# State-space rounds of a hybrid encoder block: the output products of one round stand right ahead of the table turns of the next

## The chip, the core and the metric

The kernel runs on one core of one Trainium2 chip. The metric is the device time in microseconds of one execution; three runs of the kernel before gave 892.14 (median), 893.0 and 890.85. The engines are TensorE (PE: matmuls and transposes), the vector engine (DVE), ScalarE (ACT), GpSimd (POOL), and SP, whose queue issues nearly all DMAs. Each engine works through its own instructions in their order; semaphores let one wait for another.

## The reference

One layer over a sequence of 1024 tokens of width 1024, float32 throughout: a combined input projection, a differential attention branch, a bidirectional state-space branch (S5), gates, and an output projection. The part that the change touches:

```python
proj = h @ w_in
q, k, v, z_a, u, z_s, g_a, g_s = jnp.split(proj, IN_OFFSETS, axis=-1)
...
bu_re = jnp.einsum('bsgh,gph->sbgp', uf, bb_re)     # 32 groups of 16 channels, 64 complex states
bu_im = jnp.einsum('bsgh,gph->sbgp', uf, bb_im)
_, _, x_re, x_im = lax.associative_scan(combine, (a_re, a_im, bu_re, bu_im), reverse=reverse, axis=0)
y = (jnp.einsum('sbgp,ghp->bsgh', x_re, c_re) - jnp.einsum('sbgp,ghp->bsgh', x_im, c_im))
...
y = forward(ug) + backward(ug) + d_skip * u
y = jax.nn.gelu(y)
y = y * jax.nn.sigmoid(y @ w_glu + b_glu)
ssm_branch = (y * jax.nn.silu(z_s)) @ w_up_ssm
```

The kernel forms the scan in chunks of 8 tokens: within a chunk by a product with a Toeplitz table `m`, across chunks by a scan on the vector engine.

## The kernel before

The state-space part runs in 8 rounds (i = 0 to 7) of 4 channel groups each, in `ssm_main`. At the same time TensorE has a large store of other work, the rest of the input projection. The function `drive` mixes the two by hand: `ssm_main` is a generator that yields numbers, and after each yield `drive` runs steps of the other work (the filler, `s1_fill`) until their costs add up to the number. One filler step is three wide matmuls (128x512, `mm`, L222), costed 0.66. The order on every engine's queue is just the order in which this code is written out; nothing rearranges it.

A round consists of:

- `stage_a`, `stage_rot` (vector engine): tables `cb` and `rr` for the next round; `stage_u` (SP): four DMAs that load `ut`, the inputs of the next round (L960). `ut` has 2 buffers, so the one for round i+1 takes the buffer of round i-1.
- `stage_c`: 8 products `w` on TensorE (`ut` with the turned table `gt`, L1009), and six operations on the vector engine that turn them by `rr`.
- `stage_s`: four scans on the vector engine.
- `stage_e` of the round before: the output products `yp` (L1055 `ut` with `m`, L1057 `z` with `cb`), emptied by ScalarE as `ys`, and stored by four DMAs from SP.
- `stage_r`, `stage_b` for the next round: ScalarE makes `rt` and the second half of `rr`; TensorE turns `cb` in 8 transposes `tp` (L970), and ScalarE copies them to `gt`.
- `stage_d`: six operations on the vector engine that make `z` (1 buffer) out of the scans.
- `stage_k` for the next round: 8 small products `kp` (L980), `kf` on ScalarE and the vector engine, a store `kd` and four loads `m` on SP.

The filler has its own traffic. A unit is 48 matmuls, 24 for each half, and writes two PSUM buffers in turn (`ps_mm`, tag `mm`, 2 buffers); ScalarE empties each half into `side`, and after the second half SP stores it (L1123). After its first three matmuls a unit calls `w_ahead`: ScalarE and the vector engine cut the weights of the next unit into a high and a low part (`wh` on ScalarE from the raw weights `wr`, then `wl` on the vector engine), and SP loads the raw weights of the unit after that (L174, 512 KB, `wr` with 2 buffers). A unit's first matmul reads `wh`, its third `wl`. All these stand in the same queues as the rounds' own instructions, in the order of the code.

The names of the yields: YA 2.75, YB 4.8, YC 3.2, YL 3.0 (L135).

Of the kernel before, what the change touches and what calls it, by code (L numbers as in the profile page):

```python
# [66 lines left out]
def tile_hybrid_block(  # L67
# [67 lines left out]
    YF, YA, YB, YC, YL = 12.0, 2.75, 4.8, 3.2, 3.0  # L135
# [772 lines left out]
    def ssm_main(t, ye):  # L908
# [14 lines left out]
        def stage_a(i):  # L923
            g = slice(4 * i, 4 * i + 4)
            cb = hb.tile([P, 2, 4, 8, 16, 2], F32, tag="cb", bufs=3, name="cb")
            tv = hb.tile([P, 4, 8, 32], F32, tag="t1", bufs=1, name="tv")
            sc = [P, 4, 8, 32]
            bv = [bc(bct[:, q, g].rearrange("p g h x -> p g (h x)"), 2, sc) for q in range(2)]
            wv = [bc(wt[:, q, :, g].rearrange("p k g -> p g k"), 3, sc) for q in range(2)]
            cf = cb[:].rearrange("p q g t h x -> p q g t (h x)")  # L930
            outer(cf[:, 0], cf[:, 1], bv[0], bv[1], wv[0], wv[1], tv)
            st_[i] = dict(cb=cb)

        def stage_rot(i):
            g = slice(4 * i, 4 * i + 4)
            rr = hb.tile([P, 2, 4, 8, 16], F32, tag="rr", bufs=2, name="rr")
            tv = hb.tile([P, 4, 8, 32], F32, tag="t1", bufs=1, name="tv")
            sr = [P, 4, 4, 16]
            rv = [bc(ra[:, q, :, g].rearrange("p k g -> p g k"), 3, sr) for q in range(2)]
            rw = [bc(rb[:, q, :, g].rearrange("p k g -> p g k"), 2, sr) for q in range(2)]  # L940
            outer(rr[:, 0, :, 4:8], rr[:, 1, :, 4:8], rv[0], rv[1], rw[0], rw[1], tv[:, :, 0:4, 0:16])
            st_[i]["rr"] = rr

        def stage_r(i):
            d = st_[i]
            rr = d["rr"]
            rt = hb.tile([P, 4, P], F32, tag="rt", bufs=2, name="rt")
            act(rt, bc(r8[:, 4 * i:4 * i + 4], 2, [P, 4, P]), AF.Copy)
            G.memset(rt[0:64, :, 0:1], 0.0)  # L949
            G.memset(rt[64:P, :, P - 1:P], 0.0)  # L950
            for q in range(2):
                f = rr[:, q].rearrange("p g a b -> p g (a b)")
                act(f[:, :, 0:64][:, :, ::-1], f[:, :, 64:P], AF.Copy, scale=1.0 - 2.0 * q)
            d["rt"] = rt

        def stage_u(i):
            ut = hb.tile([P, 4, P], F32, tag="ut", bufs=2, name="ut")
            for q in range(4):
                r0 = (4 * i + q) * 16
                SP.dma_start(out=ut[:, q, :], in_=ud[r0:r0 + 16, :].rearrange("h (t j) -> t h j", t=T))  # L960
            st_[i]["ut"] = ut

        def stage_b(i):
            d = st_[i]
            cb = d["cb"]
            gt = hb.tile([P, 2, 4, P], F32, tag="gt", bufs=1, name="gt")
            for q in range(2):
                ps = psw.tile([P, 512], F32, tag="tp", bufs=2, name="tp")
                for c4 in range(4):
                    PE.transpose(ps[:, c4 * P:c4 * P + P], cb[:, q, c4, :, :, 0].rearrange("p t h -> p (t h)"), ident)  # L970
                act(gt[:, q], ps[:].rearrange("p (c q) -> p c q", c=4), AF.Copy)
            d.update(gt=gt)
# [30 lines left out]
        def stage_c(i):  # L1003
            d = st_[i]
            gt, ut, rr = d["gt"], d["ut"], d["rr"]
            wp = [psw.tile([P, 4, P], F32, tag="w", bufs=2, name="w") for _ in range(2)]
            for q in range(2):
                for c4 in range(4):
                    PE.matmul(out=wp[q][:, c4, :], lhsT=gt[:, q, c4, :], rhs=ut[:, c4, :], start=True, stop=True)  # L1009
            rre = rr[:, 0].rearrange("p g a b -> p g (a b)")  # L1010
            rim = rr[:, 1].rearrange("p g a b -> p g (a b)")
            wv = hb.tile([P, 2, 4, P], F32, tag="wv", bufs=1, name="wv")
            t1 = hb.tile([P, 4, P], F32, tag="t1", bufs=1, name="t1")
            mul(wv[:, 0], wp[0], rre)
            mul(t1, wp[1], rim)
            add(wv[:, 0], wv[:, 0], t1)
            mul(wv[:, 1], wp[0], rim)
            mul(t1, wp[1], rre)
            sub(wv[:, 1], wv[:, 1], t1)
            d.update(wv=wv, rre=rre, rim=rim)  # L1020

        def stage_s(i):
            d = st_[i]
            wv, rt = d["wv"], d["rt"]
            sb = hb.tile([P, 2, 528], F32, tag="sb", bufs=1, name="sb")
            rf = rt[:].rearrange("p g j -> p (g j)")
            for q in range(2):
                wf = wv[:, q].rearrange("p g j -> p (g j)")
                V.tensor_tensor_scan(out=sb[0:64, q, 2:514], data0=rf[0:64], data1=wf[0:64],
                                     initial=0.0, op0=ALU.mult, op1=ALU.add)  # L1030
                V.tensor_tensor_scan(out=sb[64:P, q, 0:512][:, ::-1], data0=rf[64:P, ::-1], data1=wf[64:P, ::-1],
                                     initial=0.0, op0=ALU.mult, op1=ALU.add)
            sv = sb[:, :, 1:513].rearrange("p q (g j) -> p q g j", g=4)
            V.memset(sv[0:64, :, :, 0:1], 0.0)
            V.memset(sv[64:P, :, :, P - 1:P], 0.0)
            d.update(sv=sv)

        def stage_d(i):
            d = st_.pop(i)
            sv, rre, rim = (d[k] for k in ("sv", "rre", "rim"))  # L1040
            z = hb.tile([P, 2, 4, P], F32, tag="z", bufs=1, name="z")
            t1 = hb.tile([P, 4, P], F32, tag="t1", bufs=1, name="t1")
            mul(z[:, 0], sv[:, 0], rre)
            mul(t1, sv[:, 1], rim)
            add(z[:, 0], z[:, 0], t1)
            mul(z[:, 1], sv[:, 1], rre)
            mul(t1, sv[:, 0], rim)
            sub(z[:, 1], z[:, 1], t1)
            return d, z

        def stage_e(i, d, z):
            ut, cb, m = d["ut"], d["cb"], d["m"]
            yp = psw.tile([P, 4, P], F32, tag="y", bufs=1, name="yp")
            for c4 in range(4):
                PE.matmul(out=yp[:, c4, :], lhsT=m[:, c4, :], rhs=ut[:, c4, :], start=True, stop=False)  # L1055
                for q in range(2):
                    PE.matmul(out=yp[:, c4, :], lhsT=cb[:, q, c4, :, :, 1].rearrange("p t h -> p (t h)"),  # L1057
                              rhs=z[:, q, c4, :], start=False, stop=(q == 1))
            ys = yo.tile([P, 4, P], F32, tag="ys", bufs=2, name="ys")
            act(ys, yp, AF.Copy if i < NH - 1 else AF.Gelu_apprx_tanh)  # L1060
            for c4 in range(4):
                r0 = (4 * i + c4) * 16
                SP.dma_start(out=yd[r0:r0 + 16, :].rearrange("h (t j) -> t h j", t=T), in_=ys[:, c4, :])
# [19 lines left out]
        for i in range(NH):  # L1083
            if 0 < i < NH - 1:
                stage_a(i + 1)
                stage_u(i + 1)
            yield YA
            if 0 < i < NH - 1:
                stage_rot(i + 1)
            yield YA  # L1090
            stage_c(i)
            yield YA
            stage_s(i)
            yield YA
            if prev is not None:
                stage_e(*prev)
            if i in (3, 5, 7):
                SP.dma_start(out=ye[:, (i - 3) // 2], in_=yd[(i - 3) // 2 * P:(i - 1) // 2 * P, :])
            yield YB
            if i + 1 < NH:  # L1100
                stage_r(i + 1)
                stage_b(i + 1)
            prev = (i,) + stage_d(i)
            if i + 1 < NH:
                stage_k(i + 1)
            yield YC
# [29 lines left out]
    yep = tc.alloc_tile_pool(name="yep", bufs=1, side="left")  # L1136
    ye = yep.tile([P, 3, S], F32, name="ye")
    drive(ssm_main(tabs, ye), s1_fill)
    pools1[0][0].release()
    pools1[1].release()  # L1140
# [762 lines left out]
```

## Time and profile before

| | |
|---|---|
| median of three runs | 892.14 us (890.85 to 893.0) |
| the profiled execution | 892.95 us |
| its span, first to last instruction | 891.1 us |
| TensorE busy | 868.5 us, 97% |
| vector engine busy | 664.2 us, 75% |
| ScalarE busy | 367.6 us, 41% |
| the rounds in the span | about 118 to 347 us |

The shares are means over the whole span; the stages differ. Within the rounds the rows of TensorE follow one another, so the timelines of the other engines have to be read against the point at which TensorE takes up what they make. A row of a timeline gives the start in microseconds from the span's start, the duration, the engine, the line, what is written and read, and in brackets the idle time before it with what ended it. Two TensorE rows can overlap, since matmuls are pipelined. An instruction of SP is an issue; the transfer goes on behind it.

### The profile page before, as it was taken

The numbers are of one execution on the slowest core, as the hardware profiler recorded it, in microseconds if no ns is written. First come the engines' busy times: TensorE is split into PE (matmuls) and PEld (weight loads), VectorE is DVE, ScalarE is ACT, GpSimd is POOL, SyncE is SP. The second block draws the span as 40 slices with busy tenths as digits, with TensorE's granted clock in tenths as the row PEclk, the third lists the DMA queues.
The fourth block names the chain that finished last, engine by engine and source line by source line (L and its number), as shares of the span: only waits on it lengthen the run. The fifth ranks groups of instructions, "written<-read, shape, count | busy, mean of one in ns | idle before, by whom it ended". The sixth has DMA issues, their size and how long they took to land.

```text
span 891.1 us, 12219 instructions
## 1 busy us (share of the span) xinstructions
PE 868.5 (97%) x4528; PEld 732.1 (82%) x4528; DVE 664.2 (75%) x1264; ACT 367.6 (41%) x613; POOL 140.8 (16%) x133
## 2 busy tenths in 40 slices
PE   5999999999999999999999999999999999999996
PEld 4878888888888888877888888888888888878886
DVE  5986999979999987678456666787677675673465
ACT  6753452122232126421245555655555653332222
POOL 1001000000000000000003723544441311350000
PEclk9899899999999999999999999999999999999998
DMA  9936133044424245569361231342343116548022
GB/s 294 306 99 189 48 119 112 23 132 133 150 83 148 71 143 161 210 252 321 95 166 48 72 95 36 83 118 60 83 118 130 59 64 221 188 167 302 28 95 95
DMA packets 106829, 118.52 MB, mean 133 GB/s; under 512 B 7683, under 2 KB 87792, under 8 KB 106770
## 3 DMA queue, kind: packets, MB, share of 16 engines
q1 hardware_dynamic: 104980, 113.03, 41.3%
q10 hardware_dynamic: 1614, 4.51, 1.3%
q8 instruction: 36, 0.59, 0.3%
q0 software_dynamic: 176, 0.20, 0.1%
q14 instruction: 23, 0.19, 0.1%
HBM read 77.93 MB, written 27.20 MB: 118 GB/s over the span
## 4 chain that ended last, share of the span: by engine, by line
PE 88%; DVE 4%; DMA 2%; ACT 2%; issue 2%; POOL 1%; ACTq 0%; SPq 0%; DVEq 0%
PE mm L222 51%; PE op L1822 9%; PE pv L1498 5%; PE tp L1487 3%; PE sc L1456 3%; PE sc L1457 3%; PE yp L1057 2%; PE w L1009 2%; PE u L831 1%; DVE acc L96 1%; PE up L1656 1%; POOL pta L78 1%; PE mm L831 1%; PE xT L767 1%; PE tp L970 1%
## 5 line engine op out<-in xcount | busy, mean ns | idle before, releaser
L222 PE MATMUL mm<-hh,wh 128*128 128x512 f32 x592 | 238.2, 402 | 0.0
L222 PE MATMUL mm<-hl,wh 128*128 128x512 f32 x592 | 232.1, 392 | 0.0
L222 PE MATMUL mm<-hh,wl 128*128 128x512 f32 x592 | 231.7, 391 | 0.0
L222 PEld LDWEIGHTS mm<-hh,wl 128*128 128x128 f32 x592 | 111.7, 189 | 24.3 <-DVE wl L78 0.5
L222 PEld LDWEIGHTS mm<-hh,wh 128*128 128x128 f32 x592 | 111.9, 189 | 22.4 <-issue 1.7
L222 PEld LDWEIGHTS mm<-hl,wh 128*128 128x128 f32 x592 | 112.0, 189 | 20.1
L99 ACT ACTIVATE e<-sc,nm 128x1024 f32<-128x1024 f32 x64 | 71.1, 1114 | 59.9 <-DVE nm L1458 59.9
L1458 DVE TENSOR_REDUCE nm<-sc 128x1 f32<-128x1024 f32 x64 | 75.4, 1219 | 16.7 <-PE sc L1457 15.4
L78 DVE TENSOR_TENSOR wtl<-tp,wth 128x512 fp32r<-128x512 f32 x64 | 41.2, 686 | 55.6 <-ACT wth L99 55.6
L99 ACT ACTIVATE wh<-wr 128x1024 fp32r<-128x1024 f32 x49 | 51.6, 1056 | 58.0 <-DMA wr<-in_w_in_dram 22.7
L99 ACT ACTIVATE side<-mm 128x512 f32<-128x512 f32 x48 | 28.7, 598 | 102.6 <-PE mm L222 60.7
L78 DVE TENSOR_TENSOR wl<-wr,wh 128x1024 fp32r<-128x1024 f32 x36 | 43.9, 1223 | 28.5 <-ACT wh L99 28.4
L1822 PE MATMUL op<-woh,mh 128*128 128x512 f32 (+1 forms) x136 | 51.3, 377 | 1.2 <-ACT mh L99 1.2
L1822 PE MATMUL op<-woh,ml 128*128 128x512 f32 (+1 forms) x136 | 51.3, 377 | 0.0
L1822 PE MATMUL op<-wol,mh 128*128 128x512 f32 (+1 forms) x136 | 51.2, 377 | 0.0
L78 POOL TENSOR_TENSOR wl<-wr,wh 128x512 fp32r<-128x512 f32 x26 | 33.0, 1292 | 114.2 <-ACT wh L99 114.1
L1456 PE MATMUL sc<-kk,qq 128*128 128x512 f32 x128 | 49.9, 390 | 0.0
L1457 PE MATMUL sc<-kk,qb 128*128 128x512 f32 x128 | 49.8, 389 | 0.0
L99 ACT ACTIVATE wth<-tp 128x512 fp32r<-128x512 f32 x64 | 34.9, 597 | 32.4 <-PE tp L1487 32.4
L96 DVE SCALAR_TENSOR_TENSOR e<-e,wm 128x1024 f32<-128x1024 f32 x32 | 43.0, 1344 | 1.1
L949 POOL MEMSET rt<- 64x4 f32 x8 | 0.8, 98 | 240.8 <-ACT rt L99 240.8
L1498 PE MATMUL pv<-wth,vh 128*128 128x256 f32 x128 | 36.2, 283 | 0.0
(378 smaller groups left out, 1724.9 us busy)
## 6 DMA issues: line engine op xcount, KB each, us to landing
wr<-in_w_in_dram SPq DMA_DIRECT2D x40, 512.0 KB
wa<-in_w_ada_dram SPq DMA_DIRECT2D x16, 512.0 KB
x<-in_x_dram SPq DMA_DIRECT2D x8, 512.0 KB
gsd<-side SPq DMA_DIRECT2D x8, 512.0 KB
gad<-side SPq DMA_DIRECT2D x8, 512.0 KB
gt<-gsd SPq DMA_DIRECT2D x8, 512.0 KB
wg<-in_w_ada_dram SPq DMA_DIRECT2D x8, 512.0 KB
pad<-pt ACTq DMA_DIRECT2D x8, 512.0 KB
```

Source lines behind the costliest of these rows:

```text
L78: (e or V).tensor_tensor(out=o, in0=a, in1=b, op=op)
L96: V.scalar_tensor_tensor(out=o, in0=a, scalar=s, in1=b, op0=op0, op1=op1)
L99: A.activation(out=o, in_=i, func=f, **kw)
L222: PE.matmul(out=ps, lhsT=a[:, k, off:off + P], rhs=r[:, k, sl], start=(n == 0), stop=(n == 3 * K - 1))
L831: PE.matmul(out=upd[b, hf], lhsT=w[:, k, :], rhs=hid[r][:, k, hf * 512:hf * 512 + 512], start=first, stop=(left[b, hf] == 0))
L1009: PE.matmul(out=wp[q][:, c4, :], lhsT=gt[:, q, c4, :], rhs=ut[:, c4, :], start=True, stop=True)
L1456: PE.matmul(out=sc[:, sl], lhsT=H["qq"][:, cc, tok], rhs=H["kk"][:, cc, sl], start=True, stop=False)
L1457: PE.matmul(out=sc[:, sl], lhsT=qb_t[g // 2][:, cc, tb], rhs=H["kk"][:, cc, sl], start=False, stop=True)
L1458: V.tensor_reduce(out=nm[:, cc:cc + 1], in_=sc, axis=AX.X, op=ALU.max, negate=True)
L1487: PE.transpose(ps[:, k, :], e[:, kt * P:kt * P + P], ident)
L1498: PE.matmul(out=ps[:, 0:256], lhsT=a[:, kt, :], rhs=r[:, kt, :], start=(n == 0), stop=(n == 23))
L1822: PE.matmul(out=ps[:, 0:n], lhsT=a[:, k, tok], rhs=r[:, k, lo:lo + n], start=(i == 0), stop=(i == 23))
```

## The change

The yield YB between `stage_e` and `stage_r`/`stage_b` is joined with the yield YA ahead of `stage_e`. The numbers stay and so does the amount of filler; the filler that ran between the two stages now runs ahead of `stage_e`, and with it everything that it puts on ScalarE, the vector engine and SP.

```diff
--- before.py
+++ after.py
@@ -1091,12 +1091,11 @@
             stage_c(i)
             yield YA
             stage_s(i)
-            yield YA
+            yield YA + YB
             if prev is not None:
                 stage_e(*prev)
             if i in (3, 5, 7):
                 SP.dma_start(out=ye[:, (i - 3) // 2], in_=yd[(i - 3) // 2 * P:(i - 1) // 2 * P, :])
-            yield YB
             if i + 1 < NH:
                 stage_r(i + 1)
                 stage_b(i + 1)
```

Since a line falls away, all later lines of the kernel move up by one: the store of `side` is L1123 before and L1122 now.

TensorE, round 1, before: the last pair of the output products of round 0, with the filler behind them.

```order
L1055 MATMUL yp<-ut,m 128x128
L1057 MATMUL yp<-z,cb 128x128 x2
L222 MATMUL mm<-hh,wh 128x512
L222 MATMUL mm<-hl,wh 128x512
L222 MATMUL mm<-hh,wl 128x512
```

TensorE, the same place now: the last pair, the turns `tp` and the products `kp` of the next round, and then filler.

```order
L1055 MATMUL yp<-ut,m 128x128
L1057 MATMUL yp<-z,cb 128x128 x2
L970 MATMUL tp<-cst,cb 128x128 x8
L980 MATMUL kp<-cb,bz 32x128 x8
L222 MATMUL mm<-hh,wh 128x512
```

The 21 filler matmuls that stood between `yp` and `tp` now stand ahead of the 8 rows of `yp`; behind `tp` nothing has changed its place.

SP's queue, round 1, before, from the load of `ut` for round 2 to the store of `kf`.

```order
L960 DMA ut<-ud 128x1x128 x4
L1123 DMA zad<-side 128x1024
L174 DMA wr<-in_w_in_dram 128x8x128
L1063 DMA yd<-ys 8x16x128 x4
L1123 DMA gsd<-side 128x1024
L174 DMA wr<-in_w_in_dram 128x8x128
L989 DMA kd<-kf 128x240
```

SP's queue, the same place now.

```order
L960 DMA ut<-ud 128x1x128 x4
L1122 DMA zad<-side 128x1024
L174 DMA wr<-in_w_in_dram 128x8x128
L1122 DMA gsd<-side 128x1024
L174 DMA wr<-in_w_in_dram 128x8x128
L1063 DMA yd<-ys 8x16x128 x4
L989 DMA kd<-kf 128x240
```

The stores of `ys` moved behind the second store of `side` and the second weight load; the load of `ut` stands first in both, and it waits there for a semaphore of TensorE.

ScalarE, round 1, before, from the emptying of the output products to that of the filler's halves.

```order
L99 ACTIVATE ys<-yp 128x512
L99 ACTIVATE side<-mm 128x512
L99 ACTIVATE wh<-wr 128x1024
L99 ACTIVATE rt<-r_959 128x512
L99 ACTIVATE rr<-rr 128x4x64 x2
L99 ACTIVATE gt<-tp 128x512 x2
L99 ACTIVATE kf<-kp 128x112
L99 ACTIVATE side<-mm 128x512 x2
```

ScalarE, the same place now.

```order
L99 ACTIVATE side<-mm 128x512 x2
L99 ACTIVATE wh<-wr 128x1024
L99 ACTIVATE ys<-yp 128x512
L99 ACTIVATE rt<-r_959 128x512
L99 ACTIVATE rr<-rr 128x4x64 x2
L99 ACTIVATE gt<-tp 128x512 x2
L99 ACTIVATE kf<-kp 128x112
L99 ACTIVATE side<-mm 128x512 x2
```

`ys` moved from ahead of the emptying of one filler half and of the cut of the weights (`wh`) to behind them.

## Rows read from the trace of the kernel before

**Rows 1.** The page, its first part: busy time, share of the span, instructions.

```profile
PE 868.5 (97%) x4528; PEld 732.1 (82%) x4528; DVE 664.2 (75%) x1264; ACT 367.6 (41%) x613; POOL 140.8 (16%) x133
```

**Rows 2.** Windows: length, busy us by engine, then TensorE's clock, DMA share, GB/s.

```profile
100.00:102.00 2.00, 2.00 (x17) 1.63 (x15) 1.91 (x17) 0.58 (x1) 0.00 (x0) 0.86 0.00 0
...
102.00:108.00 6.00, 6.00 (x20) 4.86 (x20) 6.00 (x34) 2.84 (x5) 0.00 (x0) 0.50 0.01 3
...
200.00:300.00 100.00, 100.00 (x585) 85.45 (x584) 97.38 (x139) 27.09 (x49) 0.80 (x8) 1.00 0.40 121
```

**Rows 3.** Waits of the DMA queue on SP, 115:365: total us, times, longest.

```profile
SPq L960 <- PE yp L1057: 46.1, 6, 13.0
```

**Rows 4.** Timeline of SP's DMA issues, rounds 1 and 3: start us, us, instruction.

```profile
175.99 2.44 SPq L960 DMA_DIRECT2D ut<-ud  x4
...
178.97 0.43 SPq L174 DMA_DIRECT2D wr<-in_w_in_dram  x1
...
230.58 0.43 SPq L174 DMA_DIRECT2D wr<-in_w_in_dram  x1
```

**Rows 5.** Chain that ended last: start us, us, what. Rounds 1, 3 and 6.

```profile
176.43 4.83 PE mm L222 x21
...
228.07 5.51 PE mm L222 x24
...
306.55 4.83 PE mm L222 x21
```

**Rows 6.** Timeline of ScalarE (ACT), rounds 1, 2, 3 and 6: start us, us, instruction.

```profile
176.46 0.60 ACT L99 ACTIVATE ys<-yp 128x512 f32<-128x512 f32 x1 [7.57 <-PE yp L1057]
...
184.42 1.06 ACT L99 ACTIVATE wh<-wr 128x1024 fp32r<-128x1024 f32 x1 [6.87 <-DMA wr<-in_w_in_dram]
...
187.61 0.61 ACT L99 ACTIVATE side<-mm 128x512 f32<-128x512 f32 x1
...
213.87 0.61 ACT L99 ACTIVATE side<-mm 128x512 f32<-128x512 f32 x1
...
235.59 1.06 ACT L99 ACTIVATE wh<-wr 128x1024 fp32r<-128x1024 f32 x1 [2.06 <-DMA wr<-in_w_in_dram]
...
237.68 1.06 ACT L99 ACTIVATE gt<-tp 128x512 f32<-128x512 f32 x2
...
317.93 0.61 ACT L99 ACTIVATE side<-mm 128x512 f32<-128x512 f32 x1
```

**Rows 7.** Timeline of TensorE (PE), rounds 1 to 6: start us, us, instruction.

```profile
173.50 0.38 PE L1055 MATMUL yp<-ut,m 128*128 128x128 f32 x2
...
176.18 0.49 PE L222 MATMUL mm<-hh,wh 128*128 128x512 f32 x1
...
189.01 0.39 PE L222 MATMUL mm<-hh,wh 128*128 128x512 f32 x1
...
204.98 0.39 PE L222 MATMUL mm<-hh,wl 128*128 128x512 f32 x1
...
217.21 0.39 PE L222 MATMUL mm<-hh,wh 128*128 128x512 f32 x1
...
244.06 0.49 PE L1009 MATMUL w<-ut,gt 128*128 128x128 f32 x3
...
291.39 0.39 PE L222 MATMUL mm<-hh,wl 128*128 128x512 f32 x1
...
319.13 0.39 PE L222 MATMUL mm<-hh,wh 128*128 128x512 f32 x1
```

**Rows 8.** Timeline of the vector engine (DVE), its `wl`, rounds 1 to 5.

```profile
185.51 1.23 DVE L78 TENSOR_TENSOR wl<-wr,wh 128x1024 fp32r<-128x1024 f32 x1 [6.09 <-ACT wh L99]
...
201.30 1.22 DVE L78 TENSOR_TENSOR wl<-wr,wh 128x1024 fp32r<-128x1024 f32 x1
...
237.76 1.23 DVE L78 TENSOR_TENSOR wl<-wr,wh 128x1024 fp32r<-128x1024 f32 x1
...
288.72 1.23 DVE L78 TENSOR_TENSOR wl<-wr,wh 128x1024 fp32r<-128x1024 f32 x1
```

## The prediction

> **What bounds the kernel now.** I read the page first, then the stretches, the waits, and last the timelines of the rounds. TensorE is busy 97% of the span [rows 1]; in the middle of the state-space rounds it is busy all of 200 to 300 us at full clock, with the vector engine at 97% beside it [rows 2]. So time can be won here only by making TensorE's own row of instructions shorter, and it is lost wherever TensorE comes to stand still. What matters is therefore how far its suppliers are ahead of it. The waits of the DMA queue on SP show where they start from: 46.1 us, in 6 waits, are spent at the load of `ut` until products `yp` are done on TensorE [rows 3]. `ut` has two buffers; the load for round i+1 goes into the buffer that `stage_e(i-1)` still reads. It stands in the queue ahead of the weight load, so **stage_e on TensorE opens the gate for the weights**.
>
> In round 1 that reads: `ut` issued at 175.99, 0.4 us after the last L1055 began, weights `wr` at 178.97 [rows 4]; the cut `wh` on ScalarE starts when they land, 184.42; behind it, in order, stand rt, rr, gt, kf and then `side`, which empties a PSUM buffer from 187.61 to 188.22 [rows 6]. TensorE wants that buffer (one of two of `mm`) at 189.01 [rows 7]. The whole chain has 0.79 us in hand.
>
> **The change, part by part.** Nothing is added or removed; the filler of YB, 4.8 units, is run before `stage_e` and no longer between it and `stage_b`.
>
> *The joint group.* After a group of small products the first wide matmul of the filler takes longer, 0.49 us at 176.18 against 0.39 at 189.01 [rows 7]. One such return goes in each of rounds 1 to 6: 6 x 0.10 = 0.6 us won. The bounds are nothing, and 6 x 0.49 = 2.9 us if the whole of that matmul were overhead. I take 0.6, what the two rows show.
>
> *stage_e later.* The filler that now goes ahead of it takes 4.83 us (21 matmuls) in rounds 1 and 6, and 5.51 (24) in round 3 [rows 5]; round 2 is taken like round 1. By so much the gate opens later, and with it `ut`, the store of `side`, `wr`, `wh` and everything in ScalarE's queue behind `wh`. Besides, `ys` moves behind the waiting `wh`: it took 0.50 us up to the next start (176.46 to 176.96; it ends after 0.60 [rows 6]). Behind the waiting `wh` on ScalarE stand ys, rt, rr, gt, kf and the emptying of PSUM, and TensorE waits for the last two. The position of everything else in TensorE's row stays, so each stall is the shift less the time in hand:
> - Round 1: hand 189.01 - 188.22 = 0.79; 4.83 + 0.50 - 0.79 = 4.54 us.
> - Round 2: `side` ends at 213.87 + 0.61 = 214.48, its buffer is wanted at 217.21 [rows 6, 7], hand 2.73; 5.33 - 2.73 = 2.60.
> - Round 3: here gt ends last, 237.68 + 1.06 = 238.74, wanted by the products `w` at 244.06 [rows 6, 7], hand 5.32; 5.51 + 0.50 - 5.32 = 0.7.
> - Round 6: 317.93 + 0.61 = 318.54 against 319.13, hand 0.59; 4.83 + 0.50 - 0.59 = 4.74.
> - Rounds 4 and 5: there ScalarE cuts the weights behind the gate so late that they have long landed; I count nothing.
>
> *The vector engine's part.* It too is in order, and its `wl` follows `wh`. In round 1 it works without a gap from 185.51 until the next `wl` ends at 201.30 + 1.22 = 202.52 [rows 8]. Shifted by 4.83 that is 207.35. TensorE wanted it at 204.98 [rows 7]; it now comes there 4.54 later, and earlier by the products, which come behind it now (173.50 to 176.18, 2.68 us, in round 1 [rows 7]): 206.84. Stall 0.5; for round 2 I take the same. From round 3 on the engine is full: `wl` at 237.76 could have begun when `wh` ended, 235.59 + 1.06 = 236.65, so it moves by 5.51 - 1.11 = 4.4; the work up to the `wl` at 288.72 follows without a gap; that one ends at 289.95, wanted at 291.39, 1.44 in hand [rows 6, 7, 8]. 4.4 - 1.44, less the 0.7 that TensorE has lost by then, is 2.3.
>
> Stalls in all: 4.54 + 0.5 + 2.60 + 0.5 + 0.7 + 2.3 + 4.74 = 15.9 us.
>
> How sure is the flight of the weights? 5.45 us from issue to `wh` in round 1, 5.01 in round 3 [rows 4, 6]. With 5.0 everywhere the three PSUM stalls shrink by 0.4 each, 1.3 us in all. Upward: a second store and a second weight load now follow at once, where four small stores came first. If they shared the engines evenly the flight could double, 3 x 5.45 = 16 us more. I take 5.45, since the DMA engines are busy only 0.40 of the time in these rounds [rows 2].
>
> *What costs nothing.* `z` has one buffer, so `stage_d` now waits for a later `stage_e`; in rounds 1 to 6 the vector engine gets there behind `wl`, about 186.7 in round 1 [rows 8], when the products would be over at about 181.1. In round 7 it may really wait, but two stretches of filler (YC, YL) lie behind it; uncovered, the price would be the 4.83 by which stage_e moved. `ys` and its stores are not needed before the next stage.
>
> *The clock.* TensorE would now stand still for 4.5 us twice. Before, it never does so in the rounds. [...] I take 3.3 for each of the two long ones and nothing for the shorter ones. Where the clock falls, TensorE comes to the vector engine's `wl` later, and the 0.5 of round 1 goes.
>
> [...]
>
> **Sum.** 15.9 stalls - 0.5 (round 1) + 2 x 3.3 - 0.6 (joint groups) = 21.4 us. On the profiled execution, 892.95 us (span 891.1 and 1.85 around it), this gives 914.3; that execution lies 0.8 above the median of 892.14, so 913.5 there. TensorE has no slack later on to give it back: 97% busy over all [rows 1].
>
> **The rivals.**
> 1. *The clock stays up.* For: TensorE goes on with full bursts after each stall. [...] 15.9 - 0.6 = 15.3 us: 907.4.
> 2. *The clock falls after the shorter stalls too* (four times). [...] 15.9 - 1.0 + 4 x 3.3 - 0.6 = 27.5: 919.6. [...]
> 3. *Not slower: the gate is not what holds the weights.* If the `ut` load were released by the products `w` of the round before and not by stage_e, moving stage_e would delay nothing, and the joint groups would be left alone: 0.6 us won, 891.5; with the upper bound of 2.9 us, 889.2. For: `ut` is read by `w` too. Against: the 6 waits on yp, 46.1 us [rows 3], and the issue at 175.99, in the middle of the last products. It would decide if the chain had over 5.3 us in hand instead of 0.6 to 2.7.
> 4. *The second store and load slow the first*: flight up to twice as long, 16 us on top of 913.5, 930.
>
> **How the numbers follow.** Forecast (two falls) 0.45; rival 1 0.20; rival 2 0.22; rival 3 0.09; rival 4 0.04. The forecast is 913.5, put at 914. With one or three falls between, the range from rival 1 with the shorter flight (907.4 - 1.3, and some slack I may have overlooked in the vector engine's part, 2.3) to rival 2 with 2 us more is 904 to 922; outside lie rival 3, rival 4 and the edges of the others. What a measurement can tell from no change is 0.2%, 1.8 us. Rival 3 with its upper bound is faster by that, 0.04; the rest of it, 0.05, is the same; slower 0.91.
>
> **What would show it.** In the profile after: TensorE idle in the rounds, some 16 us, waiting for ScalarE's `side` in rounds 1, 2 and 6, for gt in round 3 and for `wl` in between; on SP the `ut` load issued about 4.8 us later in relation to the round; `wh` waiting for its DMA with `ys` behind it; the clock at half for a few us after the long stalls. If the idle time is there and the clock stays up, rival 1 holds. If `wr` takes over 6 us to land, rival 4. If TensorE has no idle time between 170 and 340 us, the step from the gate to the weights was wrong, and with it all of this.

## The result and the profile after

The changed kernel takes 919.38 us (median of 5 runs, 916.24 to 920.68) against 892.14: ratio 1.0305, 95% interval 1.0288 to 1.0321. The forecast was 914 us, with a range of 904 to 922. The change makes the kernel slower, as forecast; the time is inside the range and 5 us above the likeliest value. The profiled execution is the fastest of the five, 916.24 us; the granted clock of the other four is .979 to .983, of this one .987. The first line below is its span and mean clock, the others are TensorE's waits from 115 to 400 us (total us, times, longest); before, none of 0.5 us or more stood there.

```profile
core 0: 914.2 us, clock 0.987
...
PE mm L222 <- ACT side L99: 15.1, 3, 5.7
PE mm L222 <- DVE wl L78: 2.6, 1, 2.6
PE w L1009 <- ACT gt L99: 1.9, 1, 1.9
PE tp L970 <- DVE cb L78: 0.6, 1, 0.6
```

One by one, from TensorE's timeline (in brackets the idle time that ends at the instruction, and what ended it):

```profile
192.69 0.79 PE L222 MATMUL mm<-hh,wh 128*128 128x512 f32 x1 [5.72 <-ACT side L99]
...
227.62 0.50 PE L222 MATMUL mm<-hh,wh 128*128 128x512 f32 x1 [3.91 <-ACT side L99]
...
258.19 2.05 PE L1009 MATMUL w<-ut,gt 128*128 128x128 f32 x16 [1.88 <-ACT gt L99]
...
308.33 0.50 PE L222 MATMUL mm<-hh,wl 128*128 128x512 f32 x1 [2.61 <-DVE wl L78]
...
341.84 0.79 PE L222 MATMUL mm<-hh,wh 128*128 128x512 f32 x1 [5.49 <-ACT side L99]
```

Together they are 19.6 us, in the rounds and at the places that were named. The gate shows in the wait of [rows 3]: the load of `ut` now waits 66.0 us in its 6 waits, not 46.1. The copy `wh` waits 78.0 us for its weights, 20.2 before (the second line shows it now, the third before).

```profile
SPq L960 <- PE yp L1057: 66.0, 6, 15.0
```
```profile
ACT wh L99 <- DMA wr<-in_w_in_dram: 78.0, 8, 16.2
```
```profile
ACT wh L99 <- DMA wr<-in_w_in_dram: 20.2, 5, 6.9
```

Round 1, first SP's DMA issues, then ScalarE, as [rows 4] and [rows 6] show it before. The second store and second weight load follow the first at once; behind the waiting `wh` stand ys, rt, rr, gt, kf and then `side`, which TensorE wants.

```profile
178.59 2.44 SPq L960 DMA_DIRECT2D ut<-ud  x4
181.13 0.40 SPq L1122 DMA_DIRECT2D zad<-side  x1
181.57 0.43 SPq L174 DMA_DIRECT2D wr<-in_w_in_dram  x1
182.10 0.99 SPq L1122 DMA_DIRECT2D zad<-side  x1
183.19 0.43 SPq L174 DMA_DIRECT2D wr<-in_w_in_dram  x1
189.92 2.49 SPq L1063 DMA_DIRECT2D yd<-ys  x4
```
```profile
188.35 1.06 ACT L99 ACTIVATE wh<-wr 128x1024 fp32r<-128x1024 f32 x1 [16.22 <-DMA wr<-in_w_in_dram]
189.32 0.58 ACT L99 ACTIVATE ys<-yp 128x512 f32<-128x512 f32 x1
...
192.03 1.10 ACT L99 ACTIVATE side<-mm 128x512 f32<-128x512 f32 x2
```

From the issue of `wr` to the start of `wh` (the flight of the weights) are 188.35 - 181.57 = 6.78 us; in [rows 4, 6] they were 184.42 - 178.97 = 5.45. The forecast had taken 5.45. Round 2 has 223.28 - 216.26 = 7.02, rounds 3 and 6 have 6.82 and 6.58; before, these three took 5.54, 5.01 and 5.68.

```profile
216.26 0.44 SPq L174 DMA_DIRECT2D wr<-in_w_in_dram  x1
```
```profile
223.28 1.06 ACT L99 ACTIVATE wh<-wr 128x1024 fp32r<-128x1024 f32 x1 [14.41 <-DMA wr<-in_w_in_dram]
```

The clock, by windows (length, busy time of PE, PEld, DVE, ACT, POOL, then TensorE's clock, DMA share, GB/s). The first window is the long stall of round 1.

```profile
186.97:192.69 5.72, 0.00 (x0) 0.00 (x1) 3.21 (x5) 4.34 (x10) 0.20 (x2) 0.89 0.50 154
191.40:198.20 6.80, 5.51 (x14) 4.34 (x15) 6.63 (x12) 2.67 (x6) 0.00 (x0) 0.50 0.18 53
...
229.00:232.40 3.40, 3.40 (x16) 3.21 (x15) 3.30 (x8) 0.00 (x0) 0.00 (x0) 0.50 0.11 36
...
341.60:345.00 3.40, 3.16 (x8) 2.49 (x9) 3.30 (x9) 1.62 (x3) 0.00 (x0) 0.50 0.14 38
...
102.00:108.00 6.00, 6.00 (x30) 4.96 (x30) 6.00 (x32) 2.85 (x5) 0.00 (x0) 1.00 0.01 3
```

TensorE's granted clock stood at half for 6.8 + 3.4 + 3.4 us in the rounds, once for each stall of over 3 us. The fall at 102 us of [rows 2] is not in this execution; of the traces below, those of e1, e3 and e7 lack it too, and those of e2, e4, e5 and e8 have it.

**The books.** Half of the time at half clock is counted as lost; (1 - clock) x span is then what a whole execution lost that way: (1 - .990) x 891.1 = 8.9 us before, (1 - .987) x 914.2 = 11.9 after. Stalls 19.6 and clock 3.0 make 22.6; the spans differ by 23.1. The same sum for the runs told below, each from its own profiled execution:

| kernel | span | over before | stalls in the rounds | clock, less 8.9 | sum |
|---|---|---|---|---|---|
| changed | 914.2 | 23.1 | 19.6 | 3.0 | 22.6 |
| e5_ys_later | 915.8 | 24.7 | 16.5 | 7.6 | 24.1 |
| e8_sp_order | 908.3 | 17.2 | 12.9 | 3.8 | 16.7 |
| e4_half | 897.7 | 6.6 | 5.1 | 1.0 | 6.1 |
| e2_before_ut3 | 891.5 | 0.4 | none | 0.0 | 0.0 |
| e1_ut3 | 888.7 | -2.4 | none | -3.6 | -3.6 |
| e7_join_c | 888.2 | -2.9 | none | -3.6 | -3.6 |
| e3_ut_later | 887.8 | -3.3 | none | -4.5 | -4.5 |

The stalls are those on side, gt and `wl` of 0.5 us and more. The sums miss the differences of the spans by 0.4 to 1.2 us. Each clock is given to three places, which is 0.45 us of the span at either end, and four kernels (the changed one, e1, e3 and e7) have one wait of 0.45 to 0.6 us for `cb` besides; within these the books close, so stalls and clock are the loss to within 1.2 us. The last three rows gain only by a fall less, which executions of the kernel before show as well (clock .988 to .995); their medians below are no different from before.

### The profile page after: what moved, and what is told of

Same layout as the page of the kernel before. It is cut to its first block, busy times and chain, and to the rows that moved or that the text cites. A ratio compares the mean times of both kernels' runs of the same rounds, so it can differ in the third digit from the quotient of the medians.

```text
span 914.2 us, 12221 instructions
## 1 busy us (share of the span) xinstructions
PE 871.5 (95%) x4528; PEld 733.0 (80%) x4528; DVE 664.6 (73%) x1264; ACT 365.8 (40%) x613; POOL 140.8 (15%) x133
## 4 chain that ended last, share of the span: by engine, by line
PE 53%; DVE 3%; ACT 2%; issue 2%; POOL 1%; DMA 1%; SPq 0%; DVEq 0%; ACTq 0%
PE mm L222 26%; PE op L1821 9%; PE pv L1497 5%; PE tp L1486 3%; PE sc L1456 3%; PE sc L1455 3%; PE up L1655 1%; POOL pta L78 1%; ACT mh L99 1%; DMA wor<-in_w_out_dram 1%; DVE sg L78 1%; DVE y2l L78 1%; ACT y2h L99 0%; DVE zt L78 0%; DMA wr<-in_w_up_ssm_dram 0%
## 5 line engine op out<-in xcount | busy, mean ns | idle before, releaser
L1457 DVE TENSOR_REDUCE nm<-sc 128x1 f32<-128x1024 f32 x64 | 75.4, 1220 | 16.6 <-PE sc L1456 15.4
```

Of the source, the lines that this page charges most:

```text
L1457: V.tensor_reduce(out=nm[:, cc:cc + 1], in_=sc, axis=AX.X, op=ALU.max, negate=True)
```

## The experiments

Theory: stage_e, now later, opens the gate for `ut`, which stands ahead of the weights in SP's queue; TensorE stops for what ScalarE does behind the late weights. Rivals: the joint group or the moved products cost time by themselves; or the size of the loss comes from elsewhere.

**e1_ut3: the gate taken away.** A third buffer for `ut`; one buffer of `ys` pays for its place.

```
-  ut = hb.tile(..., tag="ut", bufs=2, ...)
+  ut = hb.tile(..., tag="ut", bufs=3, ...)
-  ys = yo.tile(..., tag="ys", bufs=2, ...)
+  ys = yo.tile(..., tag="ys", bufs=1, ...)
```

> The changed kernel with three buffers for ut instead of two (and one instead of two for ys, to make room). Theory, the gate: the load of ut no longer waits for stage_e, so the weight load behind it in SP's queue goes out early; the waits of SP for the products yp (66.0 us in the changed kernel) are gone, TensorE has no stall in the rounds, the clock does not fall there, and the time is that of the kernel before less the 0.6 us of the joint groups: 891.5, between 890.5 and 892.5. Rival, the joint group or the later stage_e costs by itself (z, yp, ys, or ScalarE's order with ys behind wh): the stalls stay, 917 to 920.

Measured 892.06 us, ratio to before 1.0002 (0.999 to 1.0014). The order on TensorE is that of the changed kernel, and the loss is gone whole. SP no longer waits for yp at the load of `ut` (L960); its only wait of any length there is one, on `side`:

```profile
SPq L960 <- ACT side L99: 4.5, 1, 4.5
```

**e2_before_ut3: the same buffers in the kernel before.**

> The kernel before with three buffers for ut (one for ys). Theory: the wait of SP for yp (46.1 us) goes, but the chain behind it had 0.6 to 2.7 us in hand before, so TensorE gains nothing: 892, within 1 us. Rival, the gate already cost time before, by DVE or ScalarE running late: faster by 2 us or more.

Measured 892.66 us, ratio 1.0011 (1.0 to 1.0021). The third buffer is worth nothing by itself, so e1 didn't win elsewhere what the change loses. It also bounds the joint group: e1 is 0.6 us below e2, and each of the two spreads over more than 3 us from execution to execution.

**e3_ut_later: the gate as late as ever, the weights ahead of it.**

```
     stage_a(i + 1)
-    stage_u(i + 1)
...
 yield YA + YB
+if 0 < i < NH - 1:
+    stage_u(i + 1)
```

> The changed kernel with the load of ut put behind the filler ahead of stage_e in the order of the code, so that in SP's queue the weight loads and the stores of side stand ahead of it; ut itself still waits for stage_e and arrives as late as in the changed kernel. Theory, head of the queue: the weights go out early, TensorE's stalls are gone, 891.5 (890.5 to 893). Rival, ut's own lateness holds TensorE (the products w wait for it): the stalls stay, over 910.

Measured 891.72 us, ratio 1.0 (0.9989 to 1.0011). The load of `ut` still waits for stage_e, 36.1 us in 6 waits, and is issued at 178.24 in round 1, as late as in the changed kernel (178.59); but both weight loads stand ahead of it, at 164.39 and 172.17 (181.57 and 183.19 there).

```profile
164.39 0.43 SPq L174 DMA_DIRECT2D wr<-in_w_in_dram  x1
...
172.17 0.43 SPq L174 DMA_DIRECT2D wr<-in_w_in_dram  x1
178.24 2.47 SPq L960 DMA_DIRECT2D ut<-ud  x4
```

So the late `ut` costs nothing here. What costs is that a load which must wait stands in SP's queue ahead of the weight loads.

**e4_half: half of the shift.**

```
-yield YA + YB
+yield YA + YB / 2
 stage_e(*prev)
 ...
+yield YB / 2
```

> The changed kernel with half of YB put back between stage_e and stage_b: 9 matmuls (2.05 us) instead of 21 are run ahead of stage_e in rounds 1, 2 and 6, 12 (2.7 us) in round 3, and no joint group. Theory, shift less time in hand: round 1 2.05 + 0.50 - 0.79 = 1.8, round 2 nothing, round 3 nothing, round 6 1.5 to 2.0, wl in rounds 1, 2 and 5 0.5 + 0.3 + 0.2; the stores of ys again stand behind the first weight load, whose flight is 5.5 us and not the 6.6 to 7.0 of the changed kernel. In all 4.4 us, too short for the clock: 896.5 (894.5 to 898.5). Rival, the cost goes with the amount moved (half of 27 us): 905. Rival, the joint group costs: 892.

Measured 900.85 us (897.64 to 903.99), ratio 1.0111 (1.0088 to 1.0134): above the 894.5 to 898.5 that were expected, and below the rival's 905. Its stalls:

```profile
189.82 0.50 PE L222 MATMUL mm<-hh,wh 128*128 128x512 f32 x1 [1.34 <-ACT side L99]
...
293.10 0.51 PE L222 MATMUL mm<-hh,wl 128*128 128x512 f32 x1 [0.57 <-DVE wl L78]
...
324.36 0.50 PE L222 MATMUL mm<-hh,wh 128*128 128x512 f32 x1 [3.18 <-ACT side L99]
```

Rounds 1 and 6 are built alike and yet differ by 1.84 us. In both a second weight load follows the first by 1.5 us; the first takes 5.17 us in round 1 (issued 180.32, `wh` at 185.49) and 7.04 in round 6:

```profile
312.99 0.43 SPq L174 DMA_DIRECT2D wr<-in_w_in_dram  x1
313.52 0.91 SPq L1123 DMA_DIRECT2D gsd<-side  x1
314.52 0.54 SPq L174 DMA_DIRECT2D wr<-in_w_in_dram  x1
```
```profile
320.03 1.06 ACT L99 ACTIVATE wh<-wr 128x1024 fp32r<-128x1024 f32 x1 [13.72 <-DMA wr<-in_w_in_dram]
```

With these flights the sum closes: the shift of the gate (1.88 us in both rounds) plus 0.48 for `ys`, plus the change of the flight (-0.28 and +1.36), less the time in hand (0.79 and 0.59) gives 1.29 and 3.13, against 1.34 and 3.18 measured. In the profiled execution the expectation missed mainly round 6, where it had left the flight at 5.5 and had counted no fall of the clock (the trace has one of 3.4 us). Rounds 2 and 3, whose time in hand is larger than the shift, have no such stall, which speaks against a cost in proportion to the amount moved. A late gate thus had a second price in these traces, a longer flight, which varied (5.17 and 7.04 us). By the books the slower executions must have stood still longer than the profiled one: at a span of 901.8 and a clock of .988 the clock takes 10.8 - 8.9 = 1.9, which leaves some 9 us of stalls; of those executions there is no trace.

**e8_sp_order: the second store and load held back.** Only SP's order is put back; the other engines keep the changed order. What is held back is a store of `side` and the weight load behind it, both together.

```
-yield YA + YB
+yield YA
+held["on"] = True      # this filler's stores and weight loads are collected
+yield YB
 stage_e(*prev)
+flush_sp()             # and issued here, behind the stores of ys
```

> The changed kernel with one thing put back: the DMAs that the second half of the joint filler issues on SP (one store of the projection's output and the second weight load) stand behind the four stores of the state-space output again, as in the kernel before; TensorE, ScalarE and VectorE keep the changed order. The stalls of the changed kernel were longer than I had reckoned because the first weight load took 6.6 to 7.0 us from its issue to the copy that waits for it, instead of 5.45. Theory A (the second weight load, issued 1.6 us behind the first, shares the DMA engines with it): flight back to about 5.4 us, the four stalls behind it shorter by 1.2 us each, 919.4 - 4.7 = 914.7 us. Theory B (the flight is longer for another reason, such as what else is under way at that time): flight stays 6.6 to 7.0 us, stalls stay, 918.5 to 920 us; the second load is then needed later than it comes in either order. A loss is possible too: if the second weight load becomes late for its own copy, 1 to 2 us more per round.

Measured 910.59 us (909.57 to 911.25), ratio 1.0207 (1.0192 to 1.0223), 8.8 us below the changed kernel. That is theory A, with more gained than its 914.7 said: the flight came down by 1.1 to 2.1 us and not by 1.2. The flight in rounds 1, 2, 3 and 6 is 5.17, 4.95, 4.78 and 5.44 us, against 6.78, 7.02, 6.82 and 6.58 in the changed kernel. Round 1:

```profile
183.26 0.43 SPq L172 DMA_DIRECT2D wr<-in_w_in_dram  x1
190.00 2.48 SPq L1077 DMA_DIRECT2D yd<-ys  x4
192.52 0.46 SPq L177 DMA_DIRECT2D zad<-side  x1
193.08 0.39 SPq L177 DMA_DIRECT2D wr<-in_w_in_dram  x1
```
```profile
188.43 1.06 ACT L99 ACTIVATE wh<-wr 128x1024 fp32r<-128x1024 f32 x1 [14.61 <-DMA wr<-in_w_in_dram]
```

The stalls are 4.11, 1.85, none and 4.34 in those rounds, 2.60 on `wl`: 12.9 in place of 19.6.

```profile
192.77 0.67 PE L236 MATMUL mm<-hh,wh 128*128 128x512 f32 x1 [4.11 <-ACT side L99]
...
224.67 0.50 PE L236 MATMUL mm<-hh,wh 128*128 128x512 f32 x1 [1.85 <-ACT side L99]
...
336.22 0.76 PE L236 MATMUL mm<-hh,wh 128*128 128x512 f32 x1 [4.34 <-ACT side L99]
```

The two profiled executions differ by 5.9 us: 6.7 less of stalls, 0.8 more of clock. The medians differ by more, since the profiled execution of the changed kernel is its fastest. DMA shares of the 7 us from the issue of the first load, in the kernel before, the changed one and this one:

```profile
178.97:185.97 7.00, 7.00 (x49) 5.74 (x48) 0.78 (x4) 1.55 (x3) 0.00 (x0) 1.00 0.94 291
```
```profile
181.57:188.57 7.00, 5.40 (x24) 4.13 (x22) 0.00 (x0) 0.22 (x1) 0.00 (x0) 1.00 0.92 291
```
```profile
183.26:190.26 7.00, 5.40 (x24) 4.13 (x22) 0.74 (x1) 1.83 (x3) 0.00 (x0) 1.00 0.53 163
```

With the second store and load gone, the share falls to 0.53. But share and flight don't go together: before, at 0.94, the flight was 5.45 us, in the changed kernel, at 0.92, it was 6.78. Which of the two that were held back, the store or the load, slows the first load is not told apart by any run.

**e5_ys_later: the emptying of yp moved out of the chain.**

```
-stage_e(*prev)                 # products, ys, stores
+ev_y = stage_e(*prev)          # products alone
 ...
 yield YC
+ev_y()                         # ys, its four stores, and the load of ye behind them
```

> The changed kernel with the eviction of the output product (ys, ScalarE) and its four stores moved behind the next filler; the products themselves stay where they are. The eviction no longer stands between the late weight copy and the eviction of the projection (side) that TensorE waits for. In the changed kernel that chain is wh, ys, rt, rr, gt, kf, side; ys takes 0.58 us and adds 0.47 to 0.52 to the chain. Theory (only the chain's length counts): three stalls shorter by 0.5 us each, the gt one too, about 2 us in all: 917.4 us. Rival (the stall is the late weight alone, what stands behind it is hidden): 919 us. If the stores' later issue delays the reload of the output before its use, slower than 920.

Measured 916.58 us (913.35 to 917.58), 2.8 below the changed kernel. The stalls of rounds 1, 2 and 3 are 5.34, 3.33 and 1.31: shorter by 0.38, 0.58 and 0.57. Round 6 is shorter by more, 3.57 in place of 5.49, because there the load took 5.07 us (333.34 to 338.41), in the other three 6.7 to 6.9. Once the flights are set off against those of the changed kernel, 0.4 to 0.5 us are left in each of the four rounds, which is `ys`.

**e7_join_c: the joint group elsewhere.** The products follow those of stage_c at once, ahead of the filler.

```
 stage_c(i)
-yield YA
-stage_s(i)
-yield YA + YB
 stage_e(*prev)
+yield YA
+stage_s(i)
+yield YA + YB
```

> Another place for the joint group: the output products of the round before follow the local products of this round at once (one group with stage_c), ahead of the filler that the change puts between, which keeps its length and stands behind. The last reader of the second input buffer is then done some 10 us earlier than in the changed kernel and 5 us earlier than before. Theory (the reader's time alone decides, the joint group as such costs nothing): the input load stands at the queue's head for a few us at most, no stall of TensorE in the rounds, 891.5 us (890.5 to 892.5). Rival 1 (the second group's products pay their own price, or its z is late there): slower than the kernel before by the stalls on z, 2 us per round, 900 us or more. Rival 2 (fewer switches between the two kinds of work are worth something): 887 to 890 us.

Measured 890.72 us (889.9 to 893.14), ratio 0.9991 (0.998 to 1.0001): no difference that can be told. The two kinds of small products stand side by side on TensorE, and the gate opens early enough that `ut` waits 24.5 us in all:

```profile
163.11 1.95 PE L1009 MATMUL w<-ut,gt 128*128 128x128 f32 x16
164.89 0.39 PE L1055 MATMUL yp<-ut,m 128*128 128x128 f32 x2
165.12 0.63 PE L1057 MATMUL yp<-z,cb 128*128 128x128 f32 x4
```
```profile
SPq L960 <- PE yp L1057: 24.5, 6, 4.7
```

Grouping was harmless here, where the gate isn't late; it won nothing that shows. None of the seven beats the kernel before.

## Why the prediction was right, and where its size was off

- *The gate.* Right: e1 and e3 take away the loss by two different edits, and leave the changed order on TensorE.
- *The shift.* Right. In round 1 TensorE wanted its buffer 189.01 - 178.97 = 10.04 us after the weights' issue before, 186.97 - 181.57 = 5.40 now: the gate is 4.64 later in relation to the round (taken: 4.83). Rounds 2 and 6 have 4.63 and 4.64, round 3 5.33 (taken: 5.51).
- *The time in hand, and ys.* Right in rounds 1, 2 and 6: from `wh` to the end of the first `side`, 3.80 us before and some 4.28 now, is the half microsecond of `ys`. Round 1 closes: 4.64 + 0.48 + 1.33 of flight - 0.79 in hand = 5.66; measured 5.72. Rounds 2 and 6: 3.86 and 5.43; measured 3.91 and 5.49. In round 3 the time in hand was read too small: it was counted to the end of the second copy `gt`, but in the changed kernel the products start at 258.19, when the first copy is done and the second still runs (to 258.62):

```profile
257.55 1.07 ACT L99 ACTIVATE gt<-tp 128x512 f32<-128x512 f32 x2
```

Before, the first copy ended at 238.26, so the hand was 5.80 us and not 5.32; 5.33 + 0.48 + 1.81 - 5.80 = 1.82, measured 1.88. Without the longer flight this round would have had next to no stall, as in e8, and not 0.7.
- *The flight of the weights.* **The mis-sized term.** It was taken as unchanged, 5.45 us; it grew by 1.33, 1.48, 1.81 and 0.90 in rounds 1, 2, 3 and 6, 5.5 us together. Doubling was priced as rival 4, with a chance of 0.04; measured is a sixth to over a third more. By the prediction's own sign (over 6 us to land) rival 4 came in part, beside the forecast. With the second store and load held back (e8) the stalls are 4.11, 1.85, none and 4.34, against 4.54, 2.60, 0.7 and 4.74 of the working; with e8's own flights and the hand of round 3 put right, the sum gives 4.05, 1.79, none and 4.29. The arithmetic stands, its input was wrong. The reason given for 5.45 was the DMA share of 0.40 [rows 2], a mean over 100 us; in the 7 us that counted it was 0.94 before already.
- *The vector engine.* Right in round 5: 2.61, forecast 2.3. The two stalls of 0.5 in rounds 1 and 2 didn't come, since TensorE reached the place later still (one had been struck off for the clock); in e8, where it came earlier, there is one of 0.44.
- *z.* Right. Its wait appears once, beside the filler of round 7, and stands in e1 too, which loses nothing:

```profile
DVE z L78 <- PE yp L1057: 2.7, 1, 2.7
```

- *The clock.* Near in the rounds: three falls, 13.6 us at half, cost 6.8; two of 3.3 were taken. The 3.3 was the author's estimate, the loss of the fall at 102 us in [rows 2] (2 x 0.14 + 6 x 0.50); no run shows it as the price of a stall, and the three falls cost 3.4, 1.7 and 1.7. But the fall at 102 us, which the sum kept, is missing in the profiled execution, so its books show 3.0. That is luck: in this execution 4.2 us too little of stalls (19.6 against the 15.4 that went into the sum) and 3.6 too much of clock nearly cancel, and 916.24 lies 1.9 above the 914.3 of the sum. Nor was the fall at 102 us the only one in the trace before: TensorE's clock was also at half from 26.3 to 33.2 us and in the last 4.6 us. The median execution, clock .981 over 917.4, lost 17.4 to the clock, 8.5 more than before; that leaves 26.3 - 8.5 = 17.8 for stalls, though it was not traced. Stalls 2.4 above and clock 1.9 above the sum make 4.3, or 4.9 if the joint group gave none of its 0.6; the median lies 5.1 above the 914.3.
- *The joint group.* 0.6 us was taken. e1 against e2 and e7 against before allow that, and can't tell it from nothing.

Rival 2 (919.6) has the right time by half-wrong reasons: there were three falls, not four, and one stall of 2.6 us had none. Rival 3 is refuted by the 66.0 us that the load of `ut` waits for yp, and by e1 and e3: without that wait, or with the weights ahead of it, the loss is gone.

**What stays open.** Why the flight is sometimes short all the same. With the second store and load held back all four flights were 5.44 us or less; with them close behind, 8 of 10 in rounds 1, 2, 3 and 6 took 6.6 to 7.0 us, and two (e4 round 1, e5 round 6) 5.1 to 5.2. Each weight load leaves sixteen completion marks in the trace. In the changed kernel's round 1 fifteen of them come 4.5 to 5.5 us after the issue and one at 6.70; before, all come from 4.0 to 5.4. In both `wh` starts 0.08 us behind the last mark (6.78 behind 6.70, 5.45 behind 5.37). Over all nine traces, from 118 to 352 us, the last mark comes more than 6.4 us after the issue in 11 of the 14 weight loads with a store 0.5 and a load 1.5 to 1.6 us behind them, and in 6 of 106 others (the 14 loads that follow so closely are left out). So the close store and load are the usual companion of a long flight, and not the only one. What holds up the last mark, no run tells.

## What to carry to other kernels

Before moving a consumer later, ask which buffer it frees, which load waits for that buffer, and what else stands behind this load in its queue: the price is the shift less the time in hand of whatever is queued behind, and a third buffer, or the waiting load placed behind the weight loads, made it nothing here (892.06 and 891.72 us against 892.14). A move that delays a load can also make it meet others: price its flight from rows in which as much is issued right behind it, not from a mean DMA share (here the flight was 6.58 to 7.02 us, and 5.45 had been taken for a mean share of 0.40). If stalls and (1 - clock) x span add up to the difference of the spans, the loss is located, and no further term is needed; why each stall came is a matter for experiments such as e1, e3 and e8.

## What the runs showed of the hardware that was not expected

A weight load landed later where a store and a load were issued close behind it on the same queue. In rounds 1, 2, 3 and 6 the flight of a 512 KB weight load was 4.78 to 5.44 us in e8, and 6.58 to 7.02 in the changed kernel, where a 512 KB store follows it by 0.5 us and a 512 KB load by 1.5 to 1.6. Why, no run shows; what the runs show is that the earlier load landed 1.1 to 2.1 us later.

Each of the nine stalls of 3.2 to 5.7 us in these traces (changed kernel, e4, e5, e8) came with a fall of the clock to half, which lasted 3.4 or 6.8 us; of three stalls of 2.6 to 2.9 us one did, and of five of 0.6 to 1.9 us none. The one at 2.60 us, in e8:

```profile
302.20:305.60 3.40, 3.16 (x8) 2.49 (x9) 3.33 (x7) 0.63 (x1) 0.00 (x0) 0.50 0.38 137
```

In six of the nine long stalls the clock fell during the wait or within 0.2 us of its end; in the other three (changed kernel round 2, e4 and e5 round 6) the matmuls started at full clock, and it fell 1.3 to 1.5 us later. The price was 1.7 or 3.4 us for each.
